# Differential attention in a 2-layer hybrid step: combination and values of a tile between the scores of the next, carried over heads and blocks

## The chip, the cores and the metric
One core of one Trainium2 chip runs the whole program. The metric is the device time of one execution in microseconds; the kernel before was run three times, and its median is 3178.19 us. The profile is of one more execution, with one record per instruction on each engine.

## What is computed
The reference is one inference step of a 2-layer decoder over a prompt of 2048 tokens and a sample group of 64 rows. Each layer has four mixers side by side; the change is in the prompt's part of the first, differential attention:

```python
def _diff_attend(q1, q2, k1, k2, v, qpos, kpos, lam):
    scale = q1.shape[-1] ** -0.5
    visible = kpos[None, :] <= qpos[:, None]

    def probs(q, k):
        s = jnp.einsum('bqhd,bkhd->bhqk', q.astype(F32), k.astype(F32)) * scale
        return jax.nn.softmax(jnp.where(visible, s, NEG_BIG), axis=-1)

    p = probs(q1, k1) - lam * probs(q2, k2)
    return jnp.einsum('bhqk,bkhd->bqhd', p, v.astype(F32))
```

There are 4 heads; q and k have two halves of 32 columns each, the values 64. After it comes an RMS norm by head, a gate, the output projection of all four mixers, a residual and a LayerNorm.

## The kernel before
Each layer has two phases. The first makes the four mixers' inputs and three of the mixers. The second, which the change concerns, is attention of the prompt with the output projection beside it. The 2048 tokens are 16 tiles of 128 queries. They are taken in five blocks: tiles 0 to 3, 4 to 7, 8 to 11, 12 and 13, 14 and 15. Within a block the four heads follow each other, and within a head its tiles; that is 64 pairs of tile and head in a layer.

For one tile `attn_probs` makes, for each of the two halves m and for each piece of up to 1024 keys (one piece for tiles 0 to 7, two from tile 8 on):

- the scores S on TensorE (L668, and L670 which adds the causal mask to the last 128 columns) into one of two PSUM tiles of 1024 columns,
- the negated row maximum on VectorE (L672, with L674 for the second piece),
- the exponential on ScalarE (L676) into an SBUF tile P, with the row sum. There are five P tiles for the first half and three for the second.

Then it combines them: the reciprocal and factor on VectorE (L687, L688, L692), the second half scaled on ScalarE (L696, first piece of two), and one pass of VectorE per piece that leaves p1 - lam (l1 / l2) p2 in the first half's P tile (L697, L702). `attn_value` takes that by groups of four key tiles: four transposes on TensorE (L715), a copy out of PSUM on ScalarE (L717), and the value products (L720) into an accumulator X of which there is one. After the last tile of a head the accumulator is copied (L110), transposed (L731) and normed with a chain of small VectorE instructions (L737 to L742, with the root in L179 to L190).

`attention` calls `attn_probs` for a tile, then `attn_value` for the tile before it; at the end of a block it calls the last `attn_value`. The projection of a block of tiles (`out_tile`, L1336 to L1378) comes one block later in the source, with a lower priority (`POUT=-500`).

What the engines run is not the order of the source. A list scheduler with a timeline model (`schedule_with_timeline_sim=True`) takes the instructions by priority, which is their place in the source unless it is shifted, and writes the order of each engine's queue. Each engine then works through its queue in order.

Of the kernel before, what the change touches and what calls it, by code (L numbers as in the profile page):

```python
# [17 lines left out]
PSUM = bass.MemoryType.PSUM  # L18
# [50 lines left out]
def hymba_step_kernel(  # L69
# [21 lines left out]
    # order, engines and buffers: P* offsets of priority, E* / L* / R* choice of engine, the others counts and orders  # L91
# [16 lines left out]
    def cpy(k, out, in_):  # L108
        """copy by ScalarE or VectorE"""
        (nc.vector.tensor_copy if KN[k] else nc.scalar.copy)(out, in_)  # L110
# [18 lines left out]
    # pools of the phase: PSUM banks of the projections, a second bank for transposes  # L129
# [21 lines left out]
    def st(tag, dt=F32):  # L151
        """rows of 512 of the streams that run beside each other: zs slabs, ms branches, os input and output"""
        return stp.tile([P, 512], dt, tag=tag, name=nm(tag), bufs=NST[tag])

    # small columns: width by stream
# [18 lines left out]
    def rsqrt(v, M, n, who, pool=True):  # L174
        """1 / sqrt(v) in place for v [M, n] > 0: estimate from the exponent bits, three Newton steps."""
# [17 lines left out]
    def gate2(dst, t, x):  # L193
        """2 silu(x) = (tanh(x / 2) + 1) x, given t = tanh(x / 2)"""
        nc.vector.scalar_tensor_tensor(dst, t, 1.0, x, op0=ALU.add, op1=ALU.mult)  # L195

# [16 lines left out]
    # page indices: row = (layer * NPOOL + page) * 128 + partition  # L213
# [15 lines left out]
    # conditioning vectors, transposed  # L229
# [50 lines left out]
    def mod(l, Lx, part, mp, bank=None):  # L280
        """shift, 1 + scale or gate of the rows of c, features on partitions."""
        dst = (Lx.shT, Lx.sc1T, Lx.gT)[part]
        for half in range(2):
# [7 lines left out]
            # the four sums are added once features are on partitions  # L291
# [23 lines left out]
    def prep(l, Lx, hp):  # L315
        """small tensors of a layer; hp: those that only the first phase needs"""
# [19 lines left out]
        with tc.tile_pool(name=nm("prep"), reuse_waits="tile", bufs=1) as pp:  # L336
# [16 lines left out]
            # lower bound: cumulative softmax over the layers, without the first  # L353
# [18 lines left out]
            # head norms; A and D carry the 1/2 of their gate  # L372
# [4 lines left out]
            # lambda of the differential attention  # L377
# [11 lines left out]
            # convolution taps  # L389
# [7 lines left out]
            # 1/4: the halves of the swish and of the gate  # L397
# [3 lines left out]
            # spatial weights, lower triangle  # L401
# [10 lines left out]
            # 1/2 of the gate in the weights and in the bias  # L412
# [13 lines left out]
    # state kept between the groups of a layer  # L426
# [92 lines left out]
    def tok_pairs(g):  # L519
        """(first token column, global tile, number of tiles, rows, is sample)"""  # L520
        out = [(i * P, g * GT + i, 2, P, False) for i in range(0, GT, 2)]
        if g == 0:
            out.append((TG, NT, 1, NS, True))
        return out
# [19 lines left out]
    def mix(main, n, *fills):  # L544
        """main (about n steps) with each fill (generator, steps, share of main over which it is spread) in between"""
# [18 lines left out]
    # ================= A: differential attention =================  # L564
# [55 lines left out]
    def attention(l, t0, nt, Lx, ap, act=None):  # L620
        """nt tiles of queries from tile t0"""
        S = scr[l]
        prev = None
# [7 lines left out]
        for hd in range(4):  # L631
# [13 lines left out]
            for j in range(nt):  # L645
                pm = prio(KN['PPB'] if t0 else KN['PPB'], attn_probs, t0 + j, qt[:, :, j * P:(j + 1) * P], kst, ls[:, j:j + 1], Lx, ap)
                if prev is not None:
                    prio(KN['PAV'], prev)
                acc = Xt() if j == 0 else acc
                prev = (lambda *a: lambda: attn_value(*a, Lx, l, ap))(t0 + j, pm, vst, acc, ls, j, nt, hd, act)  # L650
        prev()

    def attn_probs(qi, qt, kst, l1, Lx, ap):
        """p1 - lam (l1 / l2) p2, unnormalized; l1"""
# [3 lines left out]
        Pm = []  # L658
        sizes = [min(8, nk - k0) * P for k0 in range(0, nk, 8)]
        col = lambda m, j: stt[:, m * 8 + j:m * 8 + j + 1]  # L660
        for m in range(2):
            pms = []
            for pc, n in enumerate(sizes):
# [7 lines left out]
                # negated running maximum  # L671
# [5 lines left out]
                pms.append(p)  # L677
            lt = l1 if m == 0 and npc == 1 else col(m, 2)
            if npc > 1:
                # factor of the first part, whose maximum may have been smaller  # L680
# [3 lines left out]
            Pm.append((pms, lt))  # L684
        (p1s, lt1), (p2s, lt2) = Pm
# [17 lines left out]
        return p1s  # L703

    def attn_value(qi, pm, vst, acc, ls, j4, nt, hd, act, Lx, l, ap):
        """values of even key tiles on the lower columns of the array, of odd ones on the upper"""
        nk = qi + 1
        hs = slice(hd * 64, (hd + 1) * 64)
        for c in range(0, nk, 4):
            n = min(4, nk - c)  # L710
            p1 = pm[c // 8]
# [6 lines left out]
            for j in range(n):  # L718
                e = (c + j) % 2
                nc.tensor.matmul(acc[e * 64:(e + 1) * 64, j4 * P:(j4 + 1) * P], vst[c // 4][:, j, hs], ph[:, j, :],  # L720
                                 start=(c + j < 2), stop=(c + j >= nk - 2), tile_position=(0, e * 64))
        if nk == 1:
            nc.vector.memset(acc[64:128, 0:P], 0.0)
# [4 lines left out]
        # transposed, the two halves of the columns added  # L728
# [119 lines left out]
    # ================= gates =================  # L848
# [12 lines left out]
    def gate_pair(l, g, h, ca, cb):  # L861
        """two slabs, by block of tokens: the first block is done with early"""
# [29 lines left out]
    # ================= B: spatial gate =================  # L892
# [44 lines left out]
    # ================= C: convolution =================  # L937
# [120 lines left out]
    # ================= D: HGRN2 =================  # L1058
    def d_v(l, g, h, Sx, dp):
        Sx.di = dp.tile([P, GT, 256], F32, name=nm("di"))  # L1060
        if g == 0:
            # the sample rows on both halves of the partitions
# [12 lines left out]
    def d_init(g, Sx, dp):  # L1075
        """buffers of the chain of blocks, late ones first: they take the place of the convolution's"""
# [41 lines left out]
    def d_gate(f, p, n, Lx, Sx):  # L1118
        """f in place, and 1 - f"""
# [6 lines left out]
    def d_levels(q, f, k, n, levels, dp, Sx):  # L1126
        """masked products of all levels for blocks of 64 tokens: source tokens of a pair of blocks on partitions,
        (head, pair, target token) along the row (sample: the two heads on the partition halves); the products of a
        block with the one before it are left in PSUM; leaves prefix and suffix products."""
# [7 lines left out]
        def product(s, col, A, ia, B, ib, hh, par):  # L1137
            # the row tiles of the two heads work at the same time: never in one quadrant of a bank
# [49 lines left out]
    def d_norm(po, M, nq, dst, Lx):  # L1188
        """RMS norm over the 64 value columns of each head; po: [M, nq*64] in PSUM"""
# [10 lines left out]
    def d_block(l, g, p, b, q, f, Lx, Sx, dp):  # L1200
        k = d_gate(f, p, 512, Lx, Sx)
        att, sx, E = yield from d_levels(q, f, k, 512, LEVELS + (64,), dp, Sx)
        # source tokens of a pair of blocks x target tokens; the target before the source stays zero
# [78 lines left out]
    # ================= output projection, residual, LayerNorm =================  # L1282
    def out_weights(l, op):
        """w_out in two parts, and the rows of the epilogue"""
# [16 lines left out]
    def out_gate(l, O, smpl):  # L1301
        """gate rows of the sample or of the prompt"""
# [7 lines left out]
    # order of the rows of w_out: A and D (transposed here), B and C (features on partitions already)  # L1310
    O_K = (0, 1, 6, 7, 2, 3, 4, 5)

    def out_tile(l, ti, O, last=False, act=None):
        """projection, gate, residual and LayerNorm of one tile of tokens (ti None: the sample)"""
# [5 lines left out]
        # the last tiles wait for the attention: its rows come last  # L1320
# [63 lines left out]
    # ================= the layers =================  # L1384
# [177 lines left out]
```

## Time and profile before

| what | value |
|---|---|
| three runs | 3177.78, 3178.19, 3182.76 us |
| span of the profiled execution | 3202.3 us |
| TensorE matmuls busy | 2881.2 us (90%) |
| weight loads busy (beside matmuls) | 2260.0 us (71%) |
| VectorE busy | 2280.8 us (71%) |
| ScalarE busy | 1223.5 us (38%) |
| GpSimd busy | 1122.6 us (35%) |
| attention of layer 0 | from 1070 to about 1604 us |
| attention of layer 1 | from 2629 to about 3152 us, and the end to 3202 |

The page gives no separate time for the profiled execution besides its span. Busy times are sums of durations, and a matmul's end is modelled. A wait row names the instruction that waited, what released it, the total, the count and the longest. Of the two attentions, that of layer 1 ends the program.

### The profile page before, as it was taken

How to read it: one execution, taken by the hardware profiler on the slowest of the kernel's cores; microseconds unless marked ns; L12 is line 12 of the kernel's file. 1: busy time of each engine (PE TensorE's matmuls, PEld its weight loads, DVE VectorE, ACT ScalarE, POOL GpSimd, SP SyncE). 2: the span in 40 equal slices, each digit the busy share in tenths (PEclk: the TensorE clock that was granted, in tenths of full speed). 3: DMA queues.
4: the chain of work that ended last, by engine and by line, in shares of the span. 5: the costliest groups of instructions: out<-in, count | busy, mean ns of one | idle time of the engine just before them, and what ended most of it. 6: DMA issues, size and time to landing. Idle time of an engine off the chain costs nothing. (4 is left out here: it accounts for less than half of the span.)

```text
span 3202.3 us, 56179 instructions
## 1 busy us (share of the span) xinstructions
PE 2881.2 (90%) x20888; PEld 2260.0 (71%) x20888; DVE 2280.8 (71%) x5280; ACT 1223.5 (38%) x2564; POOL 1122.6 (35%) x1173
## 2 busy tenths in 40 slices
PE   6998999898999889979879989998989888997997
PEld 4888876688864466657668878776888656765665
DVE  3666883377692599988866667833776938998897
ACT  3111223312211466676642112233122137667663
POOL 4334455333230323412343443554342431241232
PEclk9999999899999899989989999998999998998998
DMA  6122323223324754546441222232232254544652
GB/s 224 61 72 85 90 83 119 79 64 93 111 90 154 192 148 129 142 103 162 122 149 57 74 88 87 86 120 81 64 105 88 69 152 120 132 130 110 150 154 72
DMA packets 343747, 353.26 MB, mean 110 GB/s; under 512 B 59728, under 2 KB 249718, under 8 KB 343459
## 3 DMA queue, kind: packets, MB, share of 16 engines
q1 hardware_dynamic: 337330, 332.90, 36.6%
q0 software_dynamic: 6144, 16.79, 1.8%
q8 instruction: 165, 2.70, 0.4%
q14 instruction: 108, 0.88, 0.1%
HBM read 266.44 MB, written 83.33 MB: 109 GB/s over the span
## 5 line engine op out<-in xcount | busy, mean ns | idle before, releaser
L515 PE MATMUL z<-hh,wh 128*128 128x512 f32 (+1 forms) x1440 | 526.5, 366 | 20.9 <-DVE zs L195 19.1
L172 POOL TENSOR_TENSOR wl<-raw,wh 128x512 fp32r<-128x512 f32 x224 | 323.1, 1455 | 609.1 <-ACT wh L110 562.8
L517 PE MATMUL z<-hh,wl 128*128 128x512 f32 (+1 forms) x1440 | 520.1, 362 | 0.0
L516 PE MATMUL z<-hl,wh 128*128 128x512 f32 (+1 forms) x1440 | 519.0, 361 | 0.0
L506 PE MATMUL z<-wh,hh 128*128 128x256 f32 (+1 forms) x1360 | 399.2, 294 | 12.6 <-issue 4.4
L1013 DVE SCALAR_TENSOR_TENSOR acc<-glu,cw,acc 128x512 f32<-128x512 f32 x480 | 402.2, 885 | 3.2
L507 PE MATMUL z<-wl,hh 128*128 128x256 f32 (+1 forms) x1360 | 394.8, 290 | 5.9 <-issue 5.9
L676 ACT ACTIVATE P<-S,stt 128x1024 f32<-128x1024 f32 (+7 forms) x384 | 332.9, 868 | 174.3 <-DVE stt L672 124.6
L508 PE MATMUL z<-wh,hl 128*128 128x256 f32 (+1 forms) x1360 | 395.7, 291 | 3.8 <-issue 3.6
L672 DVE TENSOR_REDUCE stt<-S 128x1 f32<-128x1024 f32 (+7 forms) x384 | 344.7, 905 | 62.1 <-PE S L670 45.1
L515 PEld LDWEIGHTS z<-hh,wh 128*128 128x128 f32 x1440 | 274.1, 190 | 81.7 <-DVE zs L195 23.5
L517 PEld LDWEIGHTS z<-hh,wl 128*128 128x128 f32 x1440 | 273.9, 190 | 50.9 <-issue 12.2
L516 PEld LDWEIGHTS z<-hl,wh 128*128 128x128 f32 x1440 | 274.0, 190 | 49.5 <-issue 13.8
L110 ACT CAST wh<-raw 128x512 fp32r<-128x512 f32 x224 | 133.8, 619 | 420.4 <-DMA raw<-in_w_in_dram 279.3
L668 PE MATMUL S<-K,Q 128*128 128x512 f32 (+3 forms) x640 | 226.8, 429 | 64.2 <-ACT P L676 53.6
L506 PEld LDWEIGHTS z<-wh,hh 128*128 128x128 f32 (+1 forms) x1360 | 262.0, 193 | 23.5 <-issue 10.0
L507 PEld LDWEIGHTS z<-wl,hh 128*128 128x128 f32 (+1 forms) x1360 | 261.8, 193 | 9.3 <-issue 7.8
L508 PEld LDWEIGHTS z<-wh,hl 128*128 128x128 f32 (+1 forms) x1360 | 261.9, 193 | 7.5 <-issue 5.2
L1360 PE MATMUL z<-woh,zs 128*128 128x512 f32 (+1 forms) x480 | 200.4, 417 | 16.1 <-ACT zs L110 10.1
L715 PE MATMUL T<-cst,P 128*128 128x128 f32 x1088 | 189.6, 303 | 25.1 <-DVE P L697 19.6
L172 POOL TENSOR_TENSOR zs<-os,zs 128x512 fp32r<-128x512 f32 (+1 forms) x64 | 84.3, 1319 | 348.0 <-ACT zs L110 339.1
L720 PE MATMUL X<-ph,V 128*64 128x128 f32 x2176 | 198.3, 296 | 8.1 <-ACT ph L717 7.6
(374 smaller groups left out, 5649.0 us busy)
## 6 DMA issues: line engine op xcount, KB each, us to landing
raw<-in_w_in_dram SPq DMA_DIRECT2D x128, 256.0 KB
K<-kh SPq DMA_DIRECT2D x224, 128.0 KB
K<-kl SPq DMA_DIRECT2D x224, 128.0 KB
mw<-in_w_ada_dram SPq DMA_DIRECT2D x96, 256.0 KB
raw<-in_w_in_dram SPq DMA_DIRECT2D x192, 128.0 KB
os<-gat SPq DMA_DIRECT2D x64, 256.0 KB
gat<-zs SPq DMA_DIRECT2D x48, 256.0 KB
os<-in_x_prompt_dram SPq DMA_DIRECT2D x32, 256.0 KB
```

Of the source, the lines that this page charges most:

```text
L172: eng.tensor_tensor(out, x, hi.bitcast(F32), ALU.subtract)
L506: nc.tensor.matmul(ps, hh[:, k, tok:tok + M], wh[:, k, :], start=(k == 0), stop=False)
L507: nc.tensor.matmul(ps, hh[:, k, tok:tok + M], wl[:, k, :], start=False, stop=False)
L508: nc.tensor.matmul(ps, hl[:, k, tok:tok + M], wh[:, k, :], start=False, stop=(k == KT - 1))
L515: nc.tensor.matmul(ps, wh[:, k, ms], hh[:, k, c0:c0 + n], start=(k == 0), stop=False)
L516: nc.tensor.matmul(ps, wh[:, k, ms], hl[:, k, c0:c0 + n], start=False, stop=False)
L517: nc.tensor.matmul(ps, wl[:, k, ms], hh[:, k, c0:c0 + n], start=False, stop=(k == KT - 1))
L668: nc.tensor.matmul(s[:, o:o + w], qt[:, m, :], kst[pc * 2 + o // 512][:, m, 0:w], start=True, stop=not diag)
L672: nc.vector.tensor_reduce(col(m, pc), s[:, :n], AX.X, ALU.max, negate=True)
L676: nc.scalar.activation(p[:, :n], s[:, :n], AF.Exp, bias=col(m, pc), scale=1.0, accum_out=l1 if m == 0 and npc == 1 else col(m, 2 + pc))
L1013: nc.vector.scalar_tensor_tensor(av, src(j), Lx.cw[:, c, j:j + 1], av, op0=ALU.mult, op1=ALU.add)
L1360: nc.tensor.matmul(po[0:M], a, wh[:, k, :], start=(i == 0), stop=False)
```

## The change
`attn_probs` is split into `attn_scores`, a generator that stops after each piece, and `attn_combine`, which stops after each combined piece; `attn_value` stops after each group of four key tiles. After each stop of the scores of one tile, one step of the tile before is taken (combination first, then values); what is left is run after the scores. What is left of the last tile of a head, and of a block, is carried into the next (`pool.pend`); only the last block of a layer runs its own to the end. No instruction, tile size or buffer count is altered. The rest of the diff takes comments and docstrings out, so line numbers shift: L672 is L680 after, L674 L682, L683 L693, L687 L702, L688 L703, L692 L707, L697 L712, L702 L717, L668 L676, L670 L678, L715 L730, L720 L735, L742 L758, L1368 L1384, L1370 L1386.

```diff
 def attention(l, t0, nt, Lx, ap, act=None):
-        prev = None
+        prev = pool.pend
...
             for j in range(nt):
-                pm = prio(KN['PPB'] if t0 else KN['PPB'], attn_probs, t0 + j, qt[:, :, j * P:(j + 1) * P], kst, ls[:, j:j + 1], Lx, ap)
-                if prev is not None:
-                    prio(KN['PAV'], prev)
-                acc = Xt() if j == 0 else acc
-                prev = (lambda *a: lambda: attn_value(*a, Lx, l, ap))(t0 + j, pm, vst, acc, ls, j, nt, hd, act)
-        prev()
+                sc = attn_scores(t0 + j, qt[:, :, j * P:(j + 1) * P], kst, ls[:, j:j + 1], Lx, ap)
+                steps = iter(prev) if prev else iter(())
+                for pm in sc:
+                    next(steps, None)
+                run(steps)
+                if j == 0:
+                    acc = Xt()
+                prev = chain(attn_combine(pm, Lx), attn_value(t0 + j, pm, vst, acc, ls, j, nt, hd, act, Lx, l, ap))
+
+        pool.pend = prev
+        if act is not None:
+            run(prev)
+            pool.pend = None
...
+                A.p[m].append(p)
+                if pc < npc - 1:
+                    yield A
...
+            A.l.append(lt)
+            yield A
+
+    def attn_combine(A, Lx):
...
+            yield
...
-            pool.vst = []
+            pool.vst, pool.pend = [], None
```

The orders that the scheduler writes, at three places. In the names, a number that stays the same from row to row tells which tile it is.

First, VectorE in layer 0, head 0, tile 8 (stt_1813 before, stt_1799 after) and tile 9 (stt_1823 in both), with rows of a projection's norm (omv, smo) between. Before:

```order
L672 TENSOR_REDUCE stt_1823_12547<-S_1824_12548 128x1
L1368 BN_AGGR omv_1753_12226<-obs_1746_12163 128x2
L683 SCALAR_TENSOR_TENSOR stt_1813_12509<-stt_1813_12509 128x1
L672 TENSOR_REDUCE stt_1823_12547<-S_1826_12554 128x1
L1370 TENSOR_SCALAR smo_1754_12228<-omv_1753_12226 128x1
L687 RECIPROCAL stt_1813_12509<-stt_1813_12509 128x1
L674 TENSOR_TENSOR stt_1823_12547<-stt_1823_12547 128x1
```

Now:

```order
L680 TENSOR_REDUCE stt_1823_12541<-S_1824_12542 128x1
L1384 BN_AGGR omv_1739_12167<-obs_1732_12104 128x2
L693 SCALAR_TENSOR_TENSOR stt_1799_12450<-stt_1799_12450 128x1
L680 TENSOR_REDUCE stt_1823_12541<-S_1826_12553 128x1
L1386 TENSOR_SCALAR smo_1740_12169<-omv_1739_12167 128x1
L702 RECIPROCAL stt_1799_12450<-stt_1799_12450 128x1
L682 TENSOR_TENSOR stt_1823_12541<-stt_1823_12541 128x1
```

Nothing moved: both maxima of tile 9's first half stand ahead of tile 8's reciprocal, with which its combination begins, in both programs.

Second, VectorE in layer 0, head 1, tile 12 (stt_2248) and tile 13 (stt_2276), where the two orders part for the first time. Before:

```order
L692 TENSOR_TENSOR stt_2248_14419<-stt_2248_14419 128x1
L702 SCALAR_TENSOR_TENSOR P_2252_14432<-P_2256_14448,stt_2248_14419,P_2252_14432 128x640
L190 SCALAR_TENSOR_TENSOR smay_2109_13767<-smaa_2110_13768,smay_2109_13767 128x4
L672 TENSOR_REDUCE stt_2276_14531<-S_2279_14538 128x1
L742 TENSOR_TENSOR ms_2111_13780<-ot_2104_13757,smay_2109_13767 128x256
L672 TENSOR_REDUCE stt_2276_14531<-S_2281_14548 128x1
```

Now:

```order
L707 TENSOR_TENSOR stt_2248_14413<-stt_2248_14413 128x1
L680 TENSOR_REDUCE stt_2276_14525<-S_2279_14537 128x1
L190 SCALAR_TENSOR_TENSOR smay_2221_14292<-smaa_2222_14293,smay_2221_14292 128x4
L717 SCALAR_TENSOR_TENSOR P_2252_14431<-P_2258_14459,stt_2248_14413,P_2252_14431 128x640
L682 TENSOR_TENSOR stt_2276_14525<-stt_2276_14525 128x1
L758 TENSOR_TENSOR ms_2223_14305<-ot_2216_14282,smay_2221_14292 128x256
L680 TENSOR_REDUCE stt_2276_14525<-S_2281_14548 128x1
```

The maximum of tile 13's second piece (from S_2279) moved ahead of tile 12's combination, two rows up.

Third, TensorE in layer 1: the two score products of tile 4 in head 1 (S_4206, S_4208), and between them transposes (T) and value products (X) of head 0, whose tiles are told by their P: P_4170 is tile 4, P_4176 tile 5, P_4185 tile 6. Before:

```order
L668 MATMUL S_4206_27652<-K_4202_27640,Q_4203_27645 128x128
L670 LDWEIGHTS identb_85
L670 MATMUL S_4206_27652<-cmaskb_87,identb_85 128x128
L715 MATMUL T_4181_27556<-cst_81,P_4170_27514 128x128
L720 MATMUL X_4173_27526<-ph_4182_27558,V_4163_27490 64x128
L715 MATMUL T_4190_27590<-cst_81,P_4176_27533 128x128 x2
L720 MATMUL X_4173_27526<-ph_4189_27584,V_3946_26717 64x128 x4
L715 MATMUL T_4197_27615<-cst_81,P_4185_27567 128x128 x4
L668 MATMUL S_4208_27659<-K_4201_27635,Q_4203_27645 128x512
```

Now:

```order
L676 MATMUL S_4206_27649<-K_4202_27637,Q_4203_27642 128x128
L678 LDWEIGHTS identb_85
L678 MATMUL S_4206_27649<-cmaskb_87,identb_85 128x128
L730 MATMUL T_4197_27612<-cst_81,P_4185_27564 128x128 x4
L730 MATMUL T_4199_27623<-cst_81,P_4185_27564 128x128 x3
L735 MATMUL X_4173_27523<-ph_4198_27617,V_3946_26717 64x128 x4
L735 MATMUL X_4173_27523<-ph_4200_27627,V_4151_27442 64x128 x3
L676 MATMUL S_4208_27659<-K_4201_27632,Q_4203_27642 128x512
```

The values of tiles 4 and 5 stand further ahead now, and all of tile 6's stand before the second score product of tile 4 in head 1, where before only its first four transposes did.

## Rows read from the trace of the kernel before
**Rows 1.** The page, first lines: span, busy time by engine, share and instructions
```profile
span 3202.3 us, 56179 instructions
PE 2881.2 (90%) x20888; PEld 2260.0 (71%) x20888; DVE 2280.8 (71%) x5280; ACT 1223.5 (38%) x2564; POOL 1122.6 (35%) x1173
```
**Rows 2.** Windows: us, PE, PEld, DVE, ACT, POOL busy, PE clock, DMA, GB/s
```profile
1072.00:1425.00 353.00, 307.17 (x1902) 217.22 (x1902) 319.14 (x784) 238.42 (x537) 112.15 (x90) 0.93 0.56 144
...
1425.00:1604.00 179.00, 161.83 (x1011) 121.75 (x1012) 156.36 (x364) 115.53 (x230) 55.21 (x44) 0.94 0.56 144
2629.00:3152.00 523.00, 470.29 (x2928) 337.41 (x2927) 465.33 (x1165) 348.99 (x752) 149.27 (x116) 0.94 0.51 132
```
**Rows 3.** Windows of blocks: tiles 8 to 11 of layer 0; 0 to 3, 4 to 7 of layer 1
```profile
1208.00:1389.00 181.00, 162.99 (x1000) 117.36 (x998) 173.34 (x419) 120.26 (x263) 68.46 (x53) 0.97 0.46 126
...
2629.00:2677.00 48.00, 42.09 (x223) 27.64 (x221) 34.98 (x133) 29.93 (x91) 6.56 (x6) 0.82 0.50 142
2677.00:2754.00 77.00, 71.76 (x491) 52.38 (x490) 70.90 (x169) 53.96 (x112) 13.19 (x12) 0.96 0.50 120
```
**Rows 4.** Waits of VectorE, 1425 to 1604, then 2629 to 3152: us, times, longest
```profile
DVE stt L672 <- PE S L670: 8.3, 9, 2.4
...
DVE stt L672 <- PE S L668: 2.4, 2, 2.2
...
DVE stt L672 <- PE S L670: 22.4, 23, 2.8
DVE stt L672 <- PE S L668: 9.3, 14, 1.8
```
**Rows 5.** Waits of TensorE in the same two stretches
```profile
PE S L668 <- ACT P L676: 13.9, 8, 4.0
...
PE S L668 <- ACT P L676: 20.1, 26, 2.5
```
**Rows 6.** Timeline of VectorE, last tile of layer 1: start, us, instruction, idle before
```profile
3146.97 0.16 DVE L674 TENSOR_TENSOR stt<-stt 128x1 f32<-128x1 f32 x1
3148.59 0.22 DVE L683 SCALAR_TENSOR_TENSOR stt<-stt 128x1 f32<-128x1 f32 x1 [1.46 <-ACT stt L681]
```
**Rows 7.** Timeline of SP, one of the K issue rows: start, us
```profile
1401.71 0.77 SPq L166 DMA_DIRECT2D K<-kh  x2
```
**Rows 8.** Timeline of ScalarE: first exponential of tiles 4, 8, 12, 14, both layers
```profile
1129.60 0.80 ACT L676 ACTIVATE P<-S,stt 128x640 f32<-128x640 f32 x1
...
1207.66 1.12 ACT L676 ACTIVATE P<-S,stt 128x1024 f32<-128x1024 f32 x1
...
1389.13 1.12 ACT L676 ACTIVATE P<-S,stt 128x1024 f32<-128x1024 f32 x1
...
1477.65 1.12 ACT L676 ACTIVATE P<-S,stt 128x1024 f32<-128x1024 f32 x1 [1.64 <-DVE stt L672]
...
2677.00 0.79 ACT L676 ACTIVATE P<-S,stt 128x640 f32<-128x640 f32 x1 [0.34 <-DVE stt L672]
...
2754.05 1.12 ACT L676 ACTIVATE P<-S,stt 128x1024 f32<-128x1024 f32 x1
...
2940.45 1.12 ACT L676 ACTIVATE P<-S,stt 128x1024 f32<-128x1024 f32 x1
...
3032.69 1.11 ACT L676 ACTIVATE P<-S,stt 128x1024 f32<-128x1024 f32 x1 [0.78 <-DVE stt L672]
```
**Rows 9.** Line L692 in the whole trace: count, min/median/max ns
```profile
L692 DVE TENSOR_TENSOR stt<-stt x64: 146/159/1293, 1222.2 to 3149.3; 128x1 f32<-128x1 f32 x64
```
**Rows 10.** Timeline of TensorE in layer 1: eight value products, four transposes
```profile
2696.57 0.73 PE L720 MATMUL X<-ph,V 128*64 128x128 f32 x8
2697.23 0.66 PE L715 MATMUL T<-cst,P 128*128 128x128 f32 x4
```

More of the change, by code (lines that the diff above doesn't have):

```diff
@@ L645, in attention, with attn_scores @@
             for j in range(nt):
-                pm = prio(KN['PPB'] if t0 else KN['PPB'], attn_probs, t0 + j, qt[:, :, j * P:(j + 1) * P], kst, ls[:, j:j + 1], Lx, ap)
-                if prev is not None:
-                    prio(KN['PAV'], prev)
-                acc = Xt() if j == 0 else acc
-                prev = (lambda *a: lambda: attn_value(*a, Lx, l, ap))(t0 + j, pm, vst, acc, ls, j, nt, hd, act)
-        prev()
-    def attn_probs(qi, qt, kst, l1, Lx, ap):
+                sc = attn_scores(t0 + j, qt[:, :, j * P:(j + 1) * P], kst, ls[:, j:j + 1], Lx, ap)
[10 more added lines that the diff above has]
+            pool.pend = None
+    def attn_scores(qi, qt, kst, l1, Lx, ap):
         nk = qi + 1
@@ L657, in attn_probs @@
         stt = smp.tile([P, 16], F32, tag="stt", name=nm("stt"), bufs=3)
-        Pm = []
-        sizes = [min(8, nk - k0) * P for k0 in range(0, nk, 8)]
-        col = lambda m, j: stt[:, m * 8 + j:m * 8 + j + 1]
+        A = L()
+        A.col = col = lambda m, j: stt[:, m * 8 + j:m * 8 + j + 1]
+        A.sizes = sizes = [min(8, nk - k0) * P for k0 in range(0, nk, 8)]
+        A.p, A.l = [[], []], []
         for m in range(2):
-            pms = []
             for pc, n in enumerate(sizes):
@@ L676, in attn_probs @@
                 nc.scalar.activation(p[:, :n], s[:, :n], AF.Exp, bias=col(m, pc), scale=1.0, accum_out=l1 if m == 0 and npc == 1 else col(m, 2 + pc))
-                pms.append(p)
+                A.p[m].append(p)
+                if pc < npc - 1:
+                    yield A
             lt = l1 if m == 0 and npc == 1 else col(m, 2)
@@ L683, in attn_probs @@
                 nc.vector.scalar_tensor_tensor(lt, col(m, 2), col(m, 5), col(m, 3), op0=ALU.mult, op1=ALU.add)
-            Pm.append((pms, lt))
-        (p1s, lt1), (p2s, lt2) = Pm
+            A.l.append(lt)
+            yield A
+    def attn_combine(A, Lx):
+        col, sizes, (p1s, p2s), (lt1, lt2) = A.col, A.sizes, A.p, A.l
+        npc = len(sizes)
         r = col(0, 7)
@@ L702, in attn_probs, with attn_value @@
                 nc.vector.scalar_tensor_tensor(p1[:, :n], p2[:, :n], r, p1[:, :n], op0=ALU.mult, op1=ALU.add)
-        return p1s
-    def attn_value(qi, pm, vst, acc, ls, j4, nt, hd, act, Lx, l, ap):
+            yield
+    def attn_value(qi, A, vst, acc, ls, j4, nt, hd, act, Lx, l, ap):
         nk = qi + 1
@@ L710, in attn_value @@
             n = min(4, nk - c)
-            p1 = pm[c // 8]
+            p1 = A.p[0][c // 8]
             o = (c % 8) * P
@@ L721, in attn_value @@
                                  start=(c + j < 2), stop=(c + j >= nk - 2), tile_position=(0, e * 64))
+            yield
         if nk == 1:
```

## The prediction
> **What bounds the kernel now.** I read the page first for the engines' totals [rows 1], then cut both layers' attention out of the trace, because the change touches nothing else. TensorE is busy for 90% of the span, but the edit neither adds nor drops a matmul. In the attention the engine to look at is VectorE: 319.14 of 353 us in the first part of layer 0, 156.36 of 179 in its second part, 465.33 of 523 in layer 1 [rows 2]. In the two blocks of query tiles 8 to 11 it is at 96% (173.34 of 181 us) [rows 3]; nothing put in another order can gain more than a few us there. What VectorE still loses it loses mostly to scores: in the waits of the two later stretches the row maximum (L672) waits for the score matmuls (L670, L668) for 8.3 + 2.4 and 22.4 + 9.3 us [rows 4]. Those matmuls in turn wait for the exponential (L676) to leave one of their two PSUM tiles [rows 5].
>
> **What the edit says and what it moves.** In the source the combination and the values of a tile now come a tile later, between the scores of the next tile, also across heads and blocks. But what the engines run is the order that the scheduler writes, and the orders say that it had already done this. In the first excerpt VectorE, before, already takes two maxima of tile 9 ahead of the first combination of tile 8; the changed program has the same rows there. On all five engines the two programs differ only in line and buffer numbers until head 1 of tile 13 of layer 0. So the sum has these terms.
>
> 1. *Instructions.* None is added, removed or resized: 0.
>
> 2. *Everything before about 1425 us.* The same order on the same data: 0. This holds all of the first phase and tiles 0 to 11 of layer 0.
>
> 3. *Layer 0 from 1425 to 1604 us.* Reordered. VectorE idles 179 - 156.36 = 22.6 us there [rows 2]. The second excerpt shows the kind of move: a maximum goes ahead of a combination. Counted over tiles 12 and 13, 14 maxima of later tiles now stand ahead of a tile's reciprocal where 7 did; over tiles 14 and 15 it is 4 where 9 did. More lead and then less: I take 0.
>
> 4. *Layer 1 from 2629 to 3152 us.* Reordered from its first tile on, because the scheduler starts it from another state. VectorE idles 523 - 465.33 = 57.7 us [rows 2]. Over its 64 tiles 66 maxima stood ahead of a reciprocal, now 67: 0. With term 3 this gives the ceiling of any gain, 22.6 + 57.7 = 80 us, which would need a VectorE that never waits.
>
> 5. *The end.* After the last combination the order is the same but for small rows, so the 50 us behind 3152 stay. Between the last maximum and that combination stand some 18 more small VectorE rows than before (the root of a norm, 0.16 us each, some 3 us). Now VectorE waits there for the exponential, 1.46 us in one piece between 3146.97 and 3148.59 [rows 6]; the same rows used to follow the combination, beside the transposes. If they fill the wait, 3 - 1.46 = 1.5 us stick out; if they run while the exponential is still under way, nothing. A gain is out, as they delayed nothing where they stood. Between 0 and +1.5 us, taken as 0.
>
> 6. *Queues.* The K and Q loads keep their place by head. On SP two loads of a projection tile now stand behind eight K issues, at 0.77 us for two [rows 7], so some 3 us later, once. The projection is placed last in every queue and GpSimd, its next engine, is the emptiest of all in that stretch, 55.21 of 179 us [rows 2]: 0, at worst 3.
>
> The sum is 0, but not an exact one: some 700 us of attention run in a new order, and a new order of the same work takes a different time. How different, the trace shows by itself, since it runs the same blocks twice in orders that differ a little. From the first exponential of a block to that of the next [rows 8], tiles 4 to 7 take 1207.66 - 1129.60 = 78.1 us in layer 0 and 77.1 in layer 1; tiles 8 to 11 181.5 and 186.4; tiles 12 and 13 88.5 and 92.2. The differences are 1.0, 4.9 and 3.7 us, 3.6 in the root mean square. Seven blocks are in a new order (two in layer 0, five in layer 1); if each moves by 3.6 us either way, the total moves by 3.6 x 2.65 = 9.5 us. Part of it is luck between VectorE and GpSimd: the factor product of L692 takes 159 ns in the median and up to 1293 [rows 9], and which row is caught so changes with the order.
>
> The profiled execution has a span of 3202.3 us [rows 1], 24 us over the median of the runs, 3178.2. All terms are differences, so I put them on the median: 3178 us.
>
> **Rivals.**
> *Faster: scores keep ahead.* Where the new order puts more maxima ahead of a reciprocal, which is so in 17 of the 80 reordered tiles, VectorE has its scores earlier and waits less. If all of those waits of terms 3 and 4 went, 8.3 + 2.4 + 22.4 + 9.3 = 42.4 us [rows 4], the time would be 3136; by the share of the tiles it is 42.4 x 17 / 80 = 9 us: 3169 us. Against it: the releaser of the score matmul is the exponential that empties its PSUM tile, 13.9 and 20.1 us [rows 5], and there are two such tiles before and after. The Trainium skill (Perfetto Trace Analysis, Identifying Performance Opportunities) says that a gap that repeats on the engine that ought to be full can mean too few buffers for the next tile. By that page this wait stays and the time is 3178, and the releaser agrees with the page; it is why this rival gets no more. Chance 0.21.
>
> *Slower: values push in ahead of scores.* In the source a tile's values no longer come after the next tile's combination but between its scores, so they rank higher. The third excerpt shows it on TensorE in layer 1: ahead of the second score product of tile 4 the values of tile 6 are finished, where before those of tiles 4 and 5 were. Over tiles 0 to 7 of that layer the score matmuls that stand ahead of a tile's last value product fall from 439 to 376. These 63 are some 25 score products of two or three matmuls; each now stands behind one more group of four transposes and eight value products, 0.66 + 0.73 us [rows 10], so 25 x 1.39 = 35 us of delay. It decides where the next row of VectorE is the maximum of just these scores. VectorE idles 13.0 of 48 us in tiles 0 to 3 and 6.1 of 77 in tiles 4 to 7 [rows 3], so it mostly has other work; with a third exposed the time is 3178 + 11 = 3189 us, with all of it 3213. Chance 0.19.
>
> That the change does not do what it says is no further rival: it is the forecast, as the scheduler did the same before.
>
> **How the numbers follow.** The forecast, 3178 us, has 0.60. Its own spread of 9.5 us puts half of it within 0.2% (6.4 us, about what a measurement of this kernel can tell from no change) and a quarter on each side: 0.30 same, 0.15 faster, 0.15 slower. The faster rival gives 0.17 and 0.04 same, the slower one 0.15 and 0.04 same. Together 0.32 faster, 0.38 same, 0.30 slower. Alone, the forecast would have a range of 1.3 x 9.5 = 12 us, 3166 to 3190. With the likely half of both rivals and the ends of terms 5 and 6 it is 3160 to 3196; the far halves of the rivals stay out.
>
> **What would show it.** Right: tiles 0 to 11 of layer 0 end at the same time after the first maximum; busy VectorE time in the two later stretches within a few us of 156 and 465; the same three waits at the top; blocks that differ by 1 to 5 us with both signs. The faster rival shows as L672's waits for scores down to two thirds or less, the slower one as those waits up in tiles 0 to 7 of layer 1. I am wrong if all seven blocks move the same way, or if a wait that is small now (K loads, the two projection loads on SP, or the last tile's combination) comes to the top.

## The result, and the profile after

The changed kernel takes 3219.56 us (median of 4 runs, 3218.34 to 3220.62), the kernel before 3180.48 (4 runs, 3177.78 to 3196.72): 39 us between the medians. The ratio on record is 1.0104, 95% interval 1.0078 to 1.0129, which would be 33 us; one of the four runs of before took 3196.72 us. The kernel is slower, and its time lies outside the range of the prediction. A kernel with the same order of every engine's queue (no_block_carry below) was 24 us over before on another chip, so the size is known to some 15 us only.

First the page of the changed kernel, as [rows 1]:

```profile
span 3215.9 us, 56193 instructions
PE 2885.0 (90%) x20888; PEld 2262.1 (70%) x20888; DVE 2293.4 (71%) x5280; ACT 1224.2 (38%) x2564; POOL 1120.6 (35%) x1173
```

The spans differ by 13.6 us only, the runs by 39. To see why, cut the program at the first and last exponential of each layer's attention. Before: 1072.2 us up to attention, 524.5 of attention in layer 0, 1033.9 between, 516.5 of attention in layer 1, 55.1 to the end. After: 1064.6, 534.1, 1018.8, 544.6, 53.8. The two attentions together take 1078.7 us instead of 1041.0, which is 37.7 more. The two stretches ahead of the attentions are 22.7 us shorter, and the end another 1.3. The first of them has the same order in both programs, so its 7.6 us are chance of the execution; the second can be too, as it took 1033.9 and 1034.0 us in two profiles of the kernel before and 1017.1 in a third program with the same order there (values_one_up_layer1 below). So the sum of both attentions is the number to compare between profiles; I use it from here on.

Windows of the changed kernel over the two attentions and over layer 1's tiles 0 to 3 (columns as in [rows 2]):

```profile
1064.60:1598.70 534.10, 469.87 (x2886) 337.25 (x2887) 478.79 (x1147) 352.34 (x762) 170.86 (x134) 0.93 0.56 144
2617.50:3162.10 544.60, 471.44 (x2863) 340.23 (x2862) 461.45 (x1146) 343.36 (x744) 148.41 (x116) 0.92 0.48 127
...
2617.50:2668.10 50.60, 43.43 (x213) 29.90 (x211) 35.06 (x130) 29.27 (x92) 6.71 (x6) 0.66 0.45 129
```

The same cuts of the kernel before:

```profile
1072.20:1596.70 524.50, 461.71 (x2871) 332.95 (x2872) 469.85 (x1141) 350.75 (x758) 162.47 (x131) 0.94 0.56 145
2630.70:3147.20 516.50, 464.79 (x2889) 333.69 (x2888) 462.02 (x1158) 344.45 (x746) 149.27 (x116) 0.94 0.52 134
```

In layer 1 VectorE does the same work (461.45 against 462.02 us) in 28.1 us more; all of it is idle time. TensorE idles 73.2 us instead of 51.7 and is busy 6.6 us longer, with 26 fewer matmul records in the window. Layer 0 adds 9.6 us.

Waits of VectorE and TensorE in layer 1's attention after the change, which answer to [rows 4, 5] (total, times, longest):

```profile
DVE stt L680 <- PE S L678: 39.9, 36, 4.7
...
DVE stt L680 <- PE S L676: 9.3, 9, 5.1
...
PE S L676 <- ACT P L684: 23.9, 30, 2.7
...
PE S L676 <- DMA K<-kl: 6.5, 5, 1.8
```

The maximum waits for scores 49.2 us instead of 31.7. The scores' own wait for the exponential has grown by 3.8 us only (20.1 to 23.9), so a PSUM tile that comes free late is not the main part of it.

First exponentials of layer 1's blocks (timeline of ScalarE, as [rows 8]):

```profile
2668.09 0.80 ACT L684 ACTIVATE P<-S,stt 128x640 f32<-128x640 f32 x1
...
2747.74 1.11 ACT L684 ACTIVATE P<-S,stt 128x1024 f32<-128x1024 f32 x1 [1.43 <-DVE stt L680]
...
2933.59 1.12 ACT L684 ACTIVATE P<-S,stt 128x1024 f32<-128x1024 f32 x1
...
3038.38 1.13 ACT L684 ACTIVATE P<-S,stt 128x1024 f32<-128x1024 f32 x1
```

Tiles 4 to 7 take 79.6 us (77.1 before), 8 to 11 185.9 (186.4), 12 and 13 104.8 (92.2), 14 and 15 123.8 (114.5), 0 to 3 50.6 (46.3). Most of the loss lies in tiles 12 to 15.

**One place of it, read closely.** At the end of tiles 12 and 13, TensorE after the change (start, us, instruction, idle before it):

```profile
3027.56 0.39 PE L1378 MATMUL z<-woh,zs 128*128 128x512 f32 x1
...
3029.09 0.71 PE L676 MATMUL S<-K,Q 128*128 128x512 f32 x2
3030.50 0.47 PE L676 MATMUL S<-K,Q 128*128 128x512 f32 x1 [0.69 <-ACT ph L732]
3032.78 0.66 PE L676 MATMUL S<-K,Q 128*128 128x384 f32 x1 [1.81 <-DMA K<-kl]
3033.24 0.33 PE L678 MATMUL S<-cmaskb,identb 128*128 128x128 bf16 x1
3033.37 1.06 PE L747 MATMUL T<-cst,asb 128*128 128x64 f32 x4
3034.36 1.12 PE L735 MATMUL X<-ph,V 128*64 128x128 f32 x8
3035.41 1.97 PE L730 MATMUL T<-cst,P 128*128 128x128 f32 x8
```

And before, at the same scores:

```profile
3029.94 0.73 PE L668 MATMUL S<-K,Q 128*128 128x512 f32 x2
3030.50 0.39 PE L1361 MATMUL z<-wol,zs 128*128 128x512 f32 x1
...
3031.43 0.40 PE L1362 MATMUL z<-woh,zs 128*128 128x512 f32 x1
3031.67 0.68 PE L668 MATMUL S<-K,Q 128*128 128x512 f32 x2
3032.19 0.23 PE L670 MATMUL S<-cmaskb,identb 128*128 128x128 bf16 x1
...
3032.80 0.66 PE L720 MATMUL X<-ph,V 128*64 128x128 f32 x8
```

After the change K for the next head is late, since its buffers come free only with this head's last scores. Before, matmuls of the projection (L1360 to L1362) stand at this place, and no wait for K shows. After, the order has spent the last of them at 3027.56, TensorE stands still for 1.81 us, and what follows runs slowly: eight value products take 1.12 us instead of 0.66. Windows of 10 us show the granted clock, after:

```profile
3020.00:3030.00 10.00, 9.81 (x61) 7.37 (x61) 8.21 (x14) 7.16 (x13) 5.57 (x4) 1.00 0.76 184
3030.00:3040.00 10.00, 7.01 (x37) 5.16 (x39) 5.32 (x13) 3.38 (x8) 0.00 (x0) 0.60 0.70 185
3040.00:3050.00 10.00, 8.96 (x66) 6.32 (x65) 6.75 (x12) 6.44 (x16) 3.27 (x3) 0.88 0.16 43
```

and before:

```profile
3030.00:3040.00 10.00, 8.82 (x65) 6.13 (x63) 8.67 (x19) 7.41 (x16) 0.00 (x0) 1.00 0.74 183
```

0.5 is the level of 1.2 GHz. All of head 3 of these tiles, from its first exponential to that of tile 14, after and then before:

```profile
3005.11:3038.38 33.27, 28.04 (x141) 20.87 (x143) 27.31 (x65) 18.93 (x41) 11.32 (x8) 0.80 0.61 154
...
3006.74:3032.69 25.95, 23.91 (x123) 16.64 (x123) 23.08 (x57) 17.73 (x38) 12.03 (x8) 0.93 0.59 145
```

The head takes 7.3 us more. The gap is 1.81 of them; the clock's shortfall is 0.20 x 33.27 = 6.7 us after and 0.07 x 25.95 = 1.8 before, 4.9 more, though not all of it lies behind this gap. In a second profile of each order (no_block_carry, before_again) the same head takes 32.4 and 24.4 us at clocks of 0.90 and 1.00, with 1.69 us of wait for K: there gap and clock are 4.9 of 8.0 us. So they are the larger part, but not the whole; 18 more transposes and value products also stand in the head after the change. The Trainium skill (TensorE: Matmul & The Clock Gate, HAM oscillation — how this bites in real kernels) describes such a case: a wait for a transfer between two bursts of matmuls, after which the next burst starts at half the clock. The trace agrees in the order of events, with 1.81 us of wait and 0.60 in the window; the waits of that case are longer, and here a gap of 0.69 us stands just ahead. Added up over layer 1's attention in windows of 1 us (what is missing to 1.00 in each), the shortfall is 46.1 us after the change and 29.0 before; in the second profile of each order it is 41.0 and 25.6.

### The profile page after: what moved, and what is told of

It is laid out like the page before. It is cut to its first block, busy times and chain, and to the rows that moved or that the text cites. A ratio compares the mean times of both kernels' runs of the same rounds, so it can differ in the third digit from the quotient of the medians.

```text
span 3215.9 us, 56193 instructions
## 1 busy us (share of the span) xinstructions
PE 2885.0 (90%) x20888; PEld 2262.1 (70%) x20888; DVE 2293.4 (71%) x5280; ACT 1224.2 (38%) x2564; POOL 1120.6 (35%) x1173
## 5 line engine op out<-in xcount | busy, mean ns | idle before, releaser
L172 POOL TENSOR_TENSOR wl<-raw,wh 128x512 fp32r<-128x512 f32 x224 | 316.0, 1424 | 583.2 <-ACT wh L110 548.9
L680 DVE TENSOR_REDUCE stt<-S 128x1 f32<-128x1024 f32 (+7 forms) x384 | 344.3, 904 | 78.3 <-PE S L678 59.8
L676 PE MATMUL S<-K,Q 128*128 128x512 f32 (+3 forms) x640 | 231.0, 435 | 68.7 <-ACT P L684 53.8
L735 PE MATMUL X<-ph,V 128*64 128x128 f32 x2176 | 200.9, 297 | 13.1 <-ACT ph L732 10.8
L730 PE MATMUL T<-cst,P 128*128 128x128 f32 x1088 | 191.4, 305 | 22.7 <-DVE P L712 16.7
L732 ACT COPY ph<-T 128x512 f32<-128x512 f32 (+2 forms) x320 | 160.9, 522 | 130.2 <-PE T L730 128.7
```

The lines of the kernel that those rows point to most:

```text
L172: eng.tensor_tensor(out, x, hi.bitcast(F32), ALU.subtract)
L676: nc.tensor.matmul(s[:, o:o + w], qt[:, m, :], kst[pc * 2 + o // 512][:, m, 0:w], start=True, stop=not diag)
L680: nc.vector.tensor_reduce(col(m, pc), s[:, :n], AX.X, ALU.max, negate=True)
```

## The experiments

All numbers below are the sum of both attentions from one profile each, and the time beside that of the kernel before on the same chip (before's median is 3178 to 3201 us from chip to chip, so only times of one job are compared). Seven programs and the kernel before beside them were run once each: the four pushes that mean nothing, the push in layer 1, deferred_only and interleaved_only; so were the first pair with six K buffers, and before_again against 13 runs. The others have 4 to 12 runs. Every kernel computes the whole step.

| kernel | layer 0 | layer 1 | both | time | before, same job |
|---|---|---|---|---|---|
| before | 524.5 | 516.5 | 1041.0 | 3180.5 | |
| before_again | 527.0 | 514.5 | 1041.5 | 3206.6 | 3199.2 |
| edit_but_two_tiles | 531.7 | 512.2 | 1043.9 | 3195.5 | 3199.2 |
| changed | 534.1 | 544.6 | 1078.7 | 3219.6 | 3180.5 |
| no_block_carry | 536.0 | 540.6 | 1076.6 | 3223.0 | 3199.2 |
| edit_in_two_tiles | 539.1 | 525.2 | 1064.3 | 3219.7 | 3199.2 |
| values_one_up | 554.7 | 530.4 | 1085.1 | 3236.8 | 3196.1 |
| probs_four_up | 530.5 | 529.4 | 1059.9 | 3212.9 | 3196.1 |
| modulation_30_up | 532.7 | 526.3 | 1059.0 | 3227.4 | 3196.1 |
| changed_modulation_3_up | 532.3 | 531.1 | 1063.4 | 3218.9 | 3196.1 |
| values_one_up_layer1 | 527.1 | 534.2 | 1061.3 | 3206.0 | 3179.6 |
| deferred_only | 528.0 | 518.1 | 1046.1 | 3194.9 | 3179.6 |
| interleaved_only | 525.3 | 512.7 | 1038.0 | 3178.6 | 3179.6 |
| interleaved_only_timed | 524.1 | 519.6 | 1043.7 | 3206.0 | 3200.8 |
| six_k_before | 531.3 | 511.5 | 1042.8 | 3208.7 | 3200.1 |
| six_k_changed | 524.7 | 522.8 | 1047.5 | 3215.4 | 3200.1 |
| six_k_four_p_before | 540.7 | 515.5 | 1056.2 | 3225.1 | 3201.0 |
| six_k_four_p_changed | 538.2 | 525.6 | 1063.8 | 3221.1 | 3201.0 |
| interleaved_six_k | 524.8 | 519.7 | 1044.5 | 3215.6 | 3200.8 |

### The kernel before, profiled again

> The kernel before, unchanged, for a second profiled execution. The first one had a span of 3202.3 us where the median of the runs is 3178; the profile of the changed kernel has 3215.9 us at a median of 3219.6. If the first profile was a slow sample, this one has a span near 3176 us, and the time it lost lies outside attention, in the two first phases (0 to 1070 and 1604 to 2629 us), where the changed kernel's profile is 22 us shorter with the same work. If it was not, the span is 3200 again and the two profiles differ by 14 us only.

Measured: a span of 3204.8 us, attentions at 1041.5. The expectation of 3176 is missed, and with it the idea that the first span was an odd sample: this chip runs the kernel before at 3199.2 us in the median. What the run is good for is another thing: the attentions repeat within 0.5 us in sum, and within 2.5 us in each layer.

### The edit everywhere but in two tiles, and in these two alone

Comparing the orders with the edit switched on tile by tile shows that nearly all of it changes nothing: without head 1 of tiles 12 and 13 in layer 0, the orders are those of before but for six rows.

```diff
+    MODE = lambda l, t0, hd, j: l == 0 and t0 == 12 and hd == 1
...
                 for pm in sc:
-                    next(steps, None)
+                    if not MODE(l, t0, hd, j):
+                        next(steps, None)
+                if MODE(l, t0, hd, j):
+                    run(attn_combine(pm, Lx))
                 run(steps)
```

with `prev` the values alone where `MODE` holds; the reverse has `not (...)`.

> The edit in 126 of the 128 pairs of tile and head; the old source order in head 1 of tiles 12 and 13 of layer 0 alone. The orders of all five engines are then those of the kernel before apart from six rows. Theory A (the edit does nothing by itself; one choice of the scheduler in these two tiles set off another order of all that follows): 3178 us, within 5 us, and layer 1's attention at 516 us from first to last exponential. Theory B (the values of a tile, placed between the next tile's scores, hold these scores up on TensorE; the slower rival of the prediction): the edit stands in all of layer 1, so the time stays within 5 us of 3219 us and layer 1 at 545 us.

> The reverse: the edit in head 1 of tiles 12 and 13 of layer 0 alone, everything else as in the kernel before. The orders part from those of before at the same row as the changed kernel's, and from the changed kernel's some tiles later. Theory A: another outcome of the scheduler, so another time, somewhere between 3170 and 3230 us, and layer 1's attention not at 516 us though its source is that of before. Theory B: two tiles in 128, so 3178 us and layer 1 at 516 us.

Measured: 3195.5 us against 3199.2 (ratio of the comparable runs 0.9999, 0.998 to 1.0018), and 3219.7 (1.0063, 1.0042 to 1.0085). Windows over both attentions, first with the edit in all but two tiles:

```profile
1064.80:1596.50 531.70, 470.93 (x2871) 340.43 (x2872) 469.66 (x1141) 350.57 (x760) 162.12 (x131) 0.91 0.55 143
2624.90:3137.10 512.20, 460.54 (x2889) 331.42 (x2888) 461.92 (x1158) 343.64 (x746) 147.91 (x116) 0.95 0.51 135
```

then with the edit in these two alone:

```profile
1065.90:1605.00 539.10, 477.80 (x2909) 343.63 (x2910) 476.71 (x1157) 352.40 (x762) 169.89 (x134) 0.92 0.55 143
2623.40:3148.60 525.20, 457.61 (x2849) 328.85 (x2847) 460.80 (x1142) 343.10 (x743) 144.67 (x114) 0.94 0.49 129
```

The first has the new source in all of layer 1 and before's 512 us there; the second has before's source in all of layer 1 and 525 us. Theory B falls: values between scores cost nothing where they don't change the order. The loss comes in by one choice in layer 0 that redraws everything behind it. In time these two tiles alone cost as much as the changed kernel's order does on the same chip (1.0063 here, 1.0070 in the next run); in the attentions they give 22 of its 36 us, as this order parts from the changed kernel's again, still within tiles 12 and 13 of layer 0. Layer 1 differs because the scheduler reaches it in another state.

### The changed kernel without the carry over blocks

```diff
-        pool.pend = prev
-        if act is not None:
-            run(prev)
-            pool.pend = None
+        run(prev)
```

> The changed kernel without the carry over blocks: the last tile of each block runs its combination and values at the block's end. The orders of all five engines are those of the changed kernel, row for row. If the order is all that counts, 3219 us within 5 us. If the carry costs something by itself (a buffer held longer, which no order shows), the time falls towards 3178 us.

Measured: 3223.0 us (1.0070, 1.0049 to 1.0092), attentions at 1076.6. The carry, the boldest part of the edit, does nothing. The dear place comes back too: in the 10 us around the late K the clock is 0.58, where it was 0.60 above.

```profile
3039.00:3049.00 10.00, 7.25 (x40) 5.38 (x40) 5.63 (x13) 3.85 (x8) 0.00 (x0) 0.58 0.70 186
```

### Pushes that mean nothing

Three on the kernel before, one on the changed kernel, in the table of constants only: `PAV=0` to `1`, `PPB=0` to `4`, `PMOD=0` to `30`; `PMOD=0` to `3`.

> The kernel before with the values raised in the scheduler's priority by one place (PAV=1): nothing that a tile needs, only a push to the order. Measured as the two attentions together, first to last exponential: 1041.0, 1041.5 and 1043.9 us in the three profiles with the order of before, 1078.7 and 1076.6 in the two with that of the changed kernel, 1064.3 with the edit in two tiles alone. Theory A (any push gives another order, and the order of before is at the good end of what comes out): 1050 to 1085 us. Theory C (the interleaved source gives worse orders by its kind): 1042 us within 6, as the source is that of before.

> The kernel before with scores and combination raised by four places (PPB=4), a push in the other direction. Theory A: 1050 to 1085 us for the two attentions. Theory C: 1042 us within 6. If values ahead of scores are what costs, this push works against it, and 1042 or less comes out.

> The kernel before with the modulation vectors' work in the first phase of layer 0 raised by 30 places (PMOD=30). Attention's source and priorities are untouched; it starts from another state of the scheduler. Theory A: the attentions get other orders and 1050 to 1085 us. Theory C: 1042 us within 6.

> The changed kernel with the modulation raised by three places (PMOD=3): another draw from the interleaved source. Theory A: 1050 to 1085 us, as likely below 1077 as above. Theory C: 1077 us within 6.

Measured: 1085.1, 1059.9, 1059.0 and 1063.4 us. All four lie where theory A put them (the first at the very edge of its range) and none where C did: before's source gives dear orders as well, the dearest of all among them. That one over both attentions:

```profile
1067.90:1622.60 554.70, 484.18 (x2895) 343.69 (x2896) 470.26 (x1151) 353.27 (x762) 174.71 (x134) 0.92 0.53 139
2643.50:3173.80 530.30, 464.12 (x2849) 332.57 (x2847) 456.56 (x1142) 343.56 (x742) 140.07 (x113) 0.94 0.48 128
```

VectorE's work is again what it was (470.26 and 456.56 us), and again the time grows by what it idles.

### A push in layer 1 alone, and the two halves of the edit

```diff
-                    prio(KN['PAV'], prev)
+                    prio(1 if l else 0, prev)
```

> The kernel before with the values raised by one place in layer 1 only. Layer 0 keeps the order of before; layer 1 has it up to head 1 of tile 7 and another one from there on. Theory A (the order of before lies at the good end by itself, stretch by stretch): layer 0 at 524 to 532 us, layer 1 tiles 0 to 3 at 44 to 46, and tiles 8 to 15 together 10 to 25 us above the 391 to 393 of before. Theory F (one early push spoils the whole program because the state it leaves is bad): without a push in layer 0 the time stays that of before, 1042 us within 6.

For the halves, the loop of the changed kernel with `pass` in place of `next(steps, None)` (deferred only), and with `run(attn_combine(pm, Lx))` ahead of a `chain` of the values alone (interleaved only):

> Half of the edit: the combination of a tile comes after the next tile's scores, in one piece with the values, with nothing between the scores. Theory A: another draw, 1045 to 1085 us for the two attentions. Theory C (one half of the edit is what costs): if it is the deferral, 1077 within 6, and then the other half has 1042.

> The other half: the combination stands behind its own scores as before, and only the value groups stand between the next tile's scores. Theory A: 1045 to 1085 us. Theory C: if the values between the scores are what costs, 1077 within 6, and the deferral alone has 1042.

Measured: 1061.3, 1046.1 and 1038.0 us. F falls, since layer 1 loses 18 us with layer 0 untouched. Where it loses is not where I said: tiles 8 to 15 take 394.1 us, 1 to 3 more than before, but tiles 4 to 7 91.8 instead of 77. There 96 of the projection's matmuls were put instead of 84, which at the 0.23 us from one to the next in the rows above is some 3 of the 15 us; the rest is not explained. This profile also has, in total, the longest wait for K in layer 1 of all:

```profile
PE S L668 <- DMA K<-kl: 11.0, 9, 2.8
```

9.9 us of it lie in tiles 12 to 15, and these take 210.6 us, 4 more than before. So a late K is not dear by itself.

C falls for the attentions: either half alone is at before's level within 5 us, both together are 36 over it. The whole of deferred_only took 15 us more than the kernel before, in one run of each, which shows no cost of that half and does not rule one out.

### Six K buffers

The close reading points at the K waits, so a sixth K buffer, paid for in two ways: `NK=6, os=3, zs=4`, and `NK=6, NP1=4`.

> The kernel before with six K buffers instead of five (NK=6), paid for with one os and one zs buffer (os=3, zs=4). In tiles 12 to 15 a head needs four K tiles, so with five buffers three of the next head's wait for the last scores of this one; TensorE then waits for K, 4.7 us in layer 0 and 3.4 in layer 1, and its clock is at 1.2 GHz for some us behind such a gap (34 and 29 us of full clock lost in the two attentions). Theory D (these waits at the head's end, with the clock behind them, are a cost of their own, whatever the order): K waits near 1 us a layer, clock loss down by a third, the two attentions at 1020 to 1035 us. Theory A: the order is drawn anew and hides such a gain: 1045 to 1080 us, with fewer K waits or not. The first phases can get longer by the two buffers taken away.

> The same edit on the changed kernel. Theory D: K waits from 4.7 and 6.5 us to near 1 each, the attentions from 1077 to 1050 to 1062 us. Theory A: 1045 to 1085 us, and the difference to the run before it of either sign.

> The kernel before with six K buffers, paid for with one P buffer of the first half (NK=6, NP1=4), so that the first phases keep their buffers and their order. If the gain seen with six K buffers (attentions at 1043 and 1047 us, where six draws with five gave 1059 to 1085) is the K wait's, this gives 1035 to 1055 us for the attentions, and 3190 to 3205 us in all beside about 3199 for the kernel before: no measurable gain over it, since its own order is a lucky one. If a fifth P buffer is worth more than the sixth K buffer, VectorE or ScalarE waits for a P tile and it is 1060 or more.

> The same on the changed kernel. If the K wait is what makes an order dear or cheap, 1035 to 1060 us for the attentions and 20 to 30 us less than the changed kernel's 3219 to 3223. If not, another draw between 1059 and 1085.

Measured: 1042.8, 1047.5, 1056.2 and 1063.8 us. The first lies between the ranges of both theories, above D's; the second lies in A's, just under D's; the third lies between the two readings of its expectation, and the last is the new draw of its own. In time none beats the kernel before; the two timed ones have 1.0066 (1.0045 to 1.0087) and 1.0059 (1.0036 to 1.0082).

### The best of them, timed, and with six K buffers

> The interleaved half alone, once more, timed. Its one profile had the two attentions at 1036.7 us, 5 below the 1042.1 of the order of before. If the time hangs on the order, the attentions come out at 1037 within 3 again, and the whole at 2 to 8 us less than the kernel before, 0.1 to 0.25%: at the edge of what can be measured. If that profile was chance, no difference, or slower.

> The interleaved half with six K buffers (NK=6, os=3, zs=4). If the sixth K buffer took a cost of its own out of every order, 1020 to 1032 us for the attentions. If it only draws another order, 1040 to 1080 us.

Measured: the interleaved half comes out at 1043.7, outside 1037 within 3 (the 1036.7 of the expectation was counted from layer 1's second exponential; from the first it is 1038.0), and at 1.0024 (1.0007 to 1.0041) of the kernel before. So the same order repeats within 6 us, and this version beats nothing. With six K buffers, TensorE's waits for K are 0.0 us in both layers, and yet:

```profile
1068.00:1592.80 524.80, 470.14 (x2893) 338.21 (x2894) 471.24 (x1157) 351.39 (x762) 173.59 (x134) 0.93 0.55 146
2621.00:3140.70 519.70, 460.58 (x2835) 328.84 (x2834) 448.70 (x1140) 340.78 (x742) 139.48 (x112) 0.93 0.49 129
```

1044.5 us, the same as with five; the whole is 1.0044 (1.0026 to 1.0062), with 70.4 us from the last exponential to the end instead of 56.1. The gain of D does not show: when K is no longer late, TensorE waits for something else, and the clock is no better (0.93). In layer 1 that is the projection's input, with five K buffers and with six:

```profile
PE z L1377 <- ACT zs L110: 3.4, 5, 1.8
...
PE z L1377 <- ACT zs L110: 12.6, 8, 4.8
```

This kernel has one zs buffer less, which may be the reason, so the test is not a clean one. The five orders with six K buffers have a mean of 1050.9 us and a standard deviation of 8.8, the nine with five (below) 1062.0 and 13.7. What a sixth K buffer is worth on the average stays open.

## Why the prediction was wrong, step by step

*Terms 1 and 2, right.* No instruction differs, and layer 0 has the order of before to tile 12. Its tiles 0 to 11 took 317.0 us before and 322.0 after; 321.0 and 324.1 in the two other profiles with before's order, so that is the spread of executions. That the scheduler had already done what the edit says was right and stronger than I put it: the edit is inert in 126 of 128 pairs. VectorE's 96% in tiles 8 to 11, which I gave for both layers, is layer 0's; in layer 1 it is 174.86 of 186.4 us, 94%.

*Terms 3 and 4, the step that failed.* Both were put at 0 because about as many maxima stood ahead of a reciprocal as before. In layer 1 that count went from 66 to 67, and VectorE's waits for scores from 31.7 to 49.2 us: it says nothing of the waits. I took 0 as the middle for a new order and 9.5 us as its spread, from blocks that ran in both layers. Those blocks differ by little, as I now read it, because they are all parts of one order, and that order is a good one. A sample from within a program says how its own stretches scatter, not where another program's order would lie. Measured over nine new orders with five K buffers (the changed kernel's and the interleaved half's two profiles averaged): 1040.9 to 1085.1 us, mean 1062.0, standard deviation 13.7, where before's three profiles have a mean of 1042.1. The middle is 20 us above before, not at it, and the spread nearly half as wide again as taken. The changed kernel, at 1077.6, is the second dearest. So 20 of its 36 us are what a new order cost here on the average, and the other 16 are the luck of the draw.

*Term 5, right:* the end is 53.8 us, 55.1 before. *Term 6, right in the wait alone:* TensorE waits for K 6.5 us in layer 1 instead of 3.4, which is the 3 us that I allowed. Before:

```profile
PE S L668 <- DMA K<-kl: 3.4, 5, 1.4
```

K did not come to the top of the waits. But one of these waits stands at the dear place above, and with the slow clock around it that place is above what I allowed.

*The faster rival* is out: waits for scores rose. That the scores' wait for the exponential stays was right; the Trainium skill's rule that named it (Perfetto Trace Analysis, Identifying Performance Opportunities) fits there, though no run here had a third PSUM tile for the scores.

*The slower rival* had the direction and a wrong mechanism. Its sign, L672's waits up in tiles 0 to 7 of layer 1, is there, but small (with L670's scores 9.6 to 14.6 us), and these tiles account for 4.3 + 2.5 of 28.1 us. As a property of the source it is refuted by the kernel that has the interleave in all of layer 1 at before's time.

*What I had called proof against me* was partly what came: not all blocks moved the same way (tiles 8 to 11 stayed), but layer 1's three worst lost 26.2 us together, with no wait of another kind on top. Slower had a chance of 0.30 in all, but of its sums only the far end of the slower rival, 3213 us, came near this size, with a mechanism that the runs refute, and the range left it out.

**What stays open.** Which rows of a new order make it dear was read at one place, not tested: no run changed one row and kept the rest of a dear order. The clock's shortfall in layer 1 goes with the time loosely (29.0 us at 516.5, 34.1 at 525.2, 46.1 at 544.6, but 41.0 at 518.1 in deferred_only and 34.1 at 530.4 in values_one_up), and it can be a result of the gaps as much as a cause.

## What to carry to other kernels

Where a list scheduler writes the queues, compare the orders first: most of a rearranged source may be inert, and one choice in one tile can move everything behind it. Price such a redraw from other orders of the same work (pushes of a priority by one to thirty places are cheap and gave 17 to 43 us here), not from the scatter within the present one; an order that stands at the good end, as before's does among these (one of nine new orders lay under it, by 1 us), loses on the average by an edit that does nothing. How before's order came about is not on record; that tuning picked it is a guess. And judge an idea by more than one draw: the interleaved half of this edit comes out 0.2% over before and the whole loses 24 to 39 us, though in the attentions neither half costs anything clear of the 6 us by which one order repeats.

## What was not expected

A priority moved by a single place lengthened the attentions by 43 us (values_one_up). The stretch up to the first exponential, in the same order, took 1060 to 1074 us from one profiled execution and chip to another; in the first pair of profiles differences outside attention hid 24 of 37.7 us. And taking every wait of TensorE for K away left attention where it was.
